# Differential attention: lambda and both softmax sums folded into one factor of the second component

## The chip, the cores and the metric

One core of a Trainium2 chip runs the whole program in one launch. The metric is device time in microseconds (us), the median of several executions.

## The reference, cut to what matters

Two layers of a backbone over 1024 latent and 256 context tokens. A part of each layer is differential attention with four heads. Each head has two components, and the second one's probabilities are subtracted with a factor lambda:

```python
s = jnp.einsum("bqhcd,bkhcd->bhcqk", q, k).astype(F32)
p = jax.nn.softmax(s, axis=-1)
w = (p[:, :, 0] - lam * p[:, :, 1]).astype(v.dtype)
o = jnp.einsum("bhqk,bkhd->bqhd", w, v)
...
return (rmsnorm(o, subln_g) * (1.0 - lam_init))
```

`rmsnorm` divides each row of o, over the 128 value channels of its head, by the root of its mean square plus NORM_EPS = 1e-6. It follows that a factor common to a whole row of w drops out, as long as NORM_EPS is multiplied by the square of that factor. In layer 0 latent and context queries are wanted, in layer 1 the latent ones alone.

## The kernel before, in words

The work of attention is cut into units: a head `hd`, a block `qb` of 256 queries and one half `qt` of it, 128 queries, against all 1280 keys. Block 0 is the context: its two halves make one unit, against 256 keys. Layer 0 has 36 units, layer 1 has 32. A software pipeline runs over steps s (the loop at L1310): in each step the operations of the list `K["ops"]` are issued, each for a unit that entered some steps before. For the unit that enters at step i:

- `qk` (L1188, step i): for each component TensorE makes 128 x 1280 scores in PSUM, a hi and a lo product of keys (L1209, L1210), VectorE takes the maximum (`tensor_reduce`, L1213), ScalarE the exponential, and adds up its row sum l as it goes (L1217). `u["l"]` holds l0 and l1 side by side.
- `weigh` (L1220, step i + 1): VectorE inverts both sums in one operation (L1223); GpSimd multiplies the second component, 128 x 1280, by 1/l1 and -lambda (L1226).
- `combine` (L1228, step i + 2): VectorE multiplies the first component by 1/l0 and adds the second (`scalar_tensor_tensor`, L1232).
- `trans` (L1234, step i + 3): TensorE transposes the ten 128 x 128 pieces (L1246); ScalarE and VectorE copy them to `wT` (L1247). The last two pieces go through the unused end of a score buffer.
- `pv` (L1249, step i + 4 of a block's second unit): 10 products with V for all 256 queries (L1256), in two parts; VectorE copies o (L1259).
- `subln` (L1262, steps i + 5 and i + 6): GpSimd squares o (L1267), TensorE sums the squares over the partitions with a matrix of ones (L1272), ScalarE takes logarithm and exponential for the root (L1274, L1275), VectorE scales o (L1279), and SyncE stores it (L1280).

While a head runs, `prep` loads the next head's K and Q and splits them into a rounded and a rest part: ScalarE rounds (`act.copy`, L139 and L1169), GpSimd subtracts (L140 in `split`, L1170), VectorE for head 0 alone. In the first steps `adaln_step` (L415) also puts matmuls of the conditioning in. Scores use two PSUM buffers, everything else on TensorE in this stage two banks.

GpSimd's instructions are held in the order in which they are written, over the whole program. On TensorE, VectorE and ScalarE the scheduler of the language chooses the order in the attention stage; the masks `cp` and `cd` fix it in other stages only. TensorE works its matmuls in fp32 here: one instruction of 256 or 128 columns in `pv` and `subln` shows as two records with a weight load each, a score product or a transpose as one.

Of the kernel before, what the change touches and what calls it, by code (L numbers as in the profile page):

```python
# [10 lines left out]
AF = mybir.ActivationFunctionType  # L11
ALU = mybir.AluOpType
AX = mybir.AxisListType

P = 128
# [8 lines left out]
EPS = 1e-6  # L24
# [52 lines left out]
def kernel(ctx: ExitStack, tc: tile.TileContext, I, out):  # L77
    nc = tc.nc
    sy = nc.sync
    dve = nc.vector  # L80
    act = nc.scalar
    pool = nc.gpsimd
    pe = nc.tensor
# [7 lines left out]
    def nm(s):  # L91
        uid[0] += 1
        return f"{s}{uid[0]}"
# [17 lines left out]
    def bank(shape, tag="b"):  # L111
        if TAGS[0] is not None:
            tag = "D" if tag == "b" else tag
            return PS[0].tile(shape, F32, tag=tag, name=nm(tag), bufs=TAGS[0][tag])
        return PS[0].tile(shape, F32, tag="b", name=nm("b"))
# [45 lines left out]
    def alternate(*gens):  # L161
        gens = list(gens)
        while gens:
            for g in list(gens):
                got = next(g, None)
                if got is None:
                    gens.remove(g)
                else:
                    yield got

    def tick(g, other, n):

        for got in g:
            run(g_lim(other, n))
            yield got
# [153 lines left out]
    ident = const.tile([P, P], F32, name="ident")  # L329
# [12 lines left out]
    ones = const.tile([P, P], F32, name="ones")  # L342
    epsc = const.tile([P, 1], F32, name="epsc")
# [38 lines left out]
    prmT, nlam = [], []  # L382
# [233 lines left out]
    for l in range(DEPTH):  # L616
        ps = bank([P, P])
        pe.transpose(ps[:, 0:NROW], prm_rows[:, l, :], ident[0:NROW, 0:NROW])
        t = const.tile([P, NROW], F32, name=nm("prm"))
# [111 lines left out]
    for l in range(DEPTH):  # L731
# [49 lines left out]
        def rgx_unit(ch):  # L781
            return conv_unit(lambda j: R_RCW + 2 * j + ch, R_RCB + ch, pt, lambda cv: RGS.__setitem__(("x", ch), cv), "xc")

        def rgg_unit(ch):
            G = rgt("G")
            RGS["g", ch] = G

            def evac(b, ps):
                s0, n = BLK[b]
                o = s0 if b == "c" else s0 + GAP  # L790
                act.activation(G[:, o:o + n], ps, AF.Gelu_apprx_tanh)

            return unit(X, ob, evac)
# [89 lines left out]
        u = alternate(rgx_unit(0), rgg_unit(0))  # L883
        put = gated(chain(*[store_h(b) for b in ("cab" if l == 0 else "b")]))
        u = tick(u, put, K["st"])
# [250 lines left out]
        def att(shape, tag, bufs=1, dt=F32, pl=None):  # L1136
            return (pl or AT[1]).tile(shape, dt, tag=tag, name=nm(tag), bufs=bufs)

        AT[0] = at0
        HD = {}  # L1140
# [37 lines left out]
        units = []  # L1178
# [9 lines left out]
        def qk(i, c, extra=None):  # L1188
# [26 lines left out]
            for a, (_, cc, _) in enumerate(parts):  # L1215
                p = pt_[cc][:, a // 2 * nk:(a // 2 + 1) * nk]
                act.activation(p, s[:, a, :], AF.Exp, bias=u["m"][:, c + a:c + a + 1], accum_out=u["l"][:, c + a:c + a + 1])  # L1217
                u["p"].append(p)

        def weigh(i):  # L1220
            u = U[i]
            n = len(u["p"])
            dve.reciprocal(u["l"][:, 0:n], u["l"][:, 0:n])  # L1223
            for a in range(1, n, 2):
                p = u["p"][a]
                pool.tensor_scalar(p, p, u["l"][:, a:a + 1], nlam[l], ALU.mult, ALU.mult)  # L1226

        def combine(i):  # L1228
            u = U[i]
            for a in range(0, len(u["p"]), 2):  # L1230
                p0, p1 = u["p"][a:a + 2]
                dve.scalar_tensor_tensor(p0, p0, u["l"][:, a:a + 1], p1, ALU.mult, ALU.add)  # L1232

        def trans(i, g, ext=None):  # L1234
            hd, qb, qt = units[i]
# [26 lines left out]
        def subln(i, part):  # L1262
            hd, qb, _ = units[i]
            o = HD["o", hd, qb]
            if part == 0:
                sq = att([P, 256], "sq", 2)
                pool.tensor_tensor(sq, o, o, ALU.mult)  # L1267
                HD["s", hd, qb] = sq
                return
            if part == 1:  # L1270
                sp_ = bank([P, 256])
                pe.matmul(sp_, ones, HD["s", hd, qb], start=True, stop=True)  # L1272
                rs = att([P, 256], "rs", 2)
                act.activation(rs, sp_, AF.Ln, scale=1.0 / P, bias=epsc)  # L1274
                act.activation(rs, rs, AF.Exp, scale=-0.5)  # L1275
                HD["r", hd, qb] = rs
                return
            rs = HD["r", hd, qb]
            dve.scalar_tensor_tensor(o, o, par[l]["gs"], rs, ALU.mult, ALU.mult)  # L1279
            sy.dma_start(mixD[4 + hd][:, qb * 256:(qb + 1) * 256], o)  # L1280
# [29 lines left out]
        for s in range(nu + 7):  # L1310
            if s < nu and s % per == 0 and units[s][0] < 3:
                todo = prep(units[s][0] + 1)
            e0 = (lambda ps=None: trans(s - 3, 2, ps)) if isu(s - 3) and units[s - 3][1] else None
            for op in K["ops"][l]:
                if op == "L0" and second(s - 5): subln(s - 5, 0)
                if op == "T0" and isu(s - 3): trans(s - 3, 0)
                if op == "T1" and isu(s - 3): trans(s - 3, 1)
                if op == "W" and isu(s - 1): weigh(s - 1)
                if op == "Q0" and isu(s): qk(s, 0, e0)
                if op == "Q1" and isu(s): qk(s, 1)  # L1320
                if op == "C" and isu(s - 2): combine(s - 2)
                if op == "P0" and second(s - 4): pv(s - 4, 0)
                if op == "P1" and second(s - 4): pv(s - 4, 1)
                if op == "E0" and e0 and not isu(s): e0()
                if op == "E1" and second(s - 5): subln(s - 5, 1)
                if op == "L2" and second(s - 6): subln(s - 6, 2)
                if op == "X" and todo: todo.pop(0)()
                if op in ("X", "Q1") and s < 3:
                    for _ in range(2):
                        adaln_step(ada1, None, True)  # L1330
            if s == 2:
                adaln_end()
# [230 lines left out]
        for fp in range(NF // 2):  # L1563
            if fp:
                t = xq.tile([P, 4, 512], F32, tag="hb", name=nm("s"), bufs=2)
# [102 lines left out]
        for d in range(0, KD, 2):  # L1668
            for b in ob:
                s0, n = BLK[b]  # L1670
# [166 lines left out]
```

## Time and profile before

| | |
|---|---|
| median of 3 runs | 3146.4 us (3146.09 to 3148.56) |
| the profiled execution's own time | 3146.0 us |
| its span in the profile | 3143.6 us |
| PE busy | 3012.1 us (96%) |
| DVE busy | 2035.5 us (65%) |
| ACT busy | 1376.6 us (44%) |
| POOL busy | 388.2 us (12%) |
| granted TensorE clock, mean | 0.982 of full speed |
| attention of layer 0 | about 468 to 706 us of the span |
| attention of layer 1 | about 2111 to 2330 us of the span |

PE is TensorE, PEld its weight loads, DVE VectorE, ACT ScalarE, POOL GpSimd, SP the queue of SyncE. Busy times are shares of the whole span and hide that a stage can have another limit than the program. Within attention three parts are told apart below: the head (the first units, beside loads and conditioning), the body, and the tail (no more scores, only the last units' transposes, value products and sub-norms).

### The profile page before, as it was taken

To read this page: it belongs to the slowest core of one execution; us is meant where nothing else is said; L and a number is where in the kernel's file an instruction comes from. 1 tells how busy PE (TensorE), PEld (TensorE's weight loads), DVE (VectorE), ACT (ScalarE), POOL (GpSimd) and SP (SyncE) were. 2 spreads that over 40 slices of the span, in tenths; PEclk is the share of its full clock that TensorE was granted. 3 is DMA by queue.
4 is the path that set the end of the run, shared out by engine and by line. 5 is a ranking of instruction groups with operands and counts; after the bars stand their busy time and mean duration, and the time that the engine had idled before them with its cause. 6 is when DMAs were issued, how large, how long until landed. Compare 5 with 4: busy or idle time off the path is not lost. (4 is left out here: it accounts for less than half of the span.)

```text
span 3143.6 us, 41895 instructions
## 1 busy us (share of the span) xinstructions
PE 3012.1 (96%) x15825; PEld 2472.4 (79%) x15825; DVE 2035.5 (65%) x3088; ACT 1376.6 (44%) x2491; POOL 388.2 (12%) x386
## 2 busy tenths in 40 slices
PE   6999998999999999999999799999989899999998
PEld 4888776778778778888888688877878688887887
DVE  5744657976764455557777664668966766666777
ACT  6643746765432323232212545746744433333122
POOL 1113114532000000000000013115421000000000
PEclk8999999999999999999999999999999999999999
DMA  9127565208233332225222224344124122225331
GB/s 310 57 79 212 176 175 143 67 17 265 69 116 127 115 122 73 81 67 198 91 76 76 70 86 124 112 137 133 39 101 151 54 81 81 81 83 197 95 94 61
DMA packets 327441, 353.11 MB, mean 112 GB/s; under 512 B 22237, under 2 KB 269382, under 8 KB 327238
## 3 DMA queue, kind: packets, MB, share of 16 engines
q1 hardware_dynamic: 327062, 350.36, 36.0%
q8 instruction: 124, 2.03, 0.3%
q14 instruction: 79, 0.65, 0.1%
q10 hardware_dynamic: 176, 0.07, 0.0%
HBM read 268.05 MB, written 82.31 MB: 111 GB/s over the span
## 5 line engine op out<-in xcount | busy, mean ns | idle before, releaser
L139 ACT CAST wo<-wr 128x512 fp32r<-128x512 f32 x374 | 230.2, 620 | 459.4 <-issue 145.2
L1464 PE MATMUL A<-x,wo 128*128 128x512 f32 x1584 | 392.2, 396 | 7.2 <-DVE wo L140 5.1
L1656 DVE SCALAR_TENSOR_TENSOR h<-b,mod,h 128x512 f32<-128x512 f32 (+1 forms) x456 | 301.4, 677 | 123.9 <-PE b L123 113.6
L140 DVE TENSOR_TENSOR wo<-wr,wo 128x512 fp32r<-128x512 f32 x374 | 253.9, 688 | 191.8 <-ACT wo L139 189.2
L1464 PEld LDWEIGHTS A<-x,wo 128*128 128x128 f32 x1584 | 294.3, 188 | 81.8 <-issue 7.5
L122 PE MATMUL b<-hl,wo 128*128 128x512 f32 (+1 forms) x912 | 333.9, 367 | 3.2 <-DVE hl L140 3.1
L121 PE MATMUL b<-hh,wo 128*128 128x512 f32 (+1 forms) x912 | 333.2, 366 | 3.6 <-ACT hh L139 3.4
L123 PE MATMUL b<-hh,wo 128*128 128x512 f32 (+1 forms) x912 | 332.3, 365 | 0.0
L123 PE MATMUL b<-xh,wl 128*128 128x512 f32 (+1 forms) x864 | 312.4, 362 | 11.6 <-DVE wl L140 11.6
L121 PE MATMUL b<-xh,wh 128*128 128x512 f32 (+1 forms) x864 | 317.9, 368 | 5.5 <-ACT xh L139 4.2
L122 PE MATMUL b<-xl,wh 128*128 128x512 f32 (+1 forms) x864 | 312.5, 362 | 7.1 <-DVE xl L490 4.2
L1464 PE MATMUL B<-x,wo 128*128 128x512 f32 x1056 | 263.9, 396 | 8.3 <-DVE x L140 5.6
L1464 PEld LDWEIGHTS B<-x,wo 128*128 128x128 f32 x1056 | 196.9, 189 | 57.8 <-DVE x L140 10.9
L1217 ACT ACTIVATE p<-s,m 128x1280 f32<-128x1280 f32 (+1 forms) x144 | 177.2, 1233 | 69.0 <-DVE m L1213 62.3
L121 PEld LDWEIGHTS b<-hh,wo 128*128 128x128 f32 x912 | 171.8, 189 | 35.8 <-ACT hh L139 5.0
L122 PEld LDWEIGHTS b<-hl,wo 128*128 128x128 f32 x912 | 172.3, 189 | 34.6 <-DVE hl L140 4.9
L1213 DVE TENSOR_REDUCE m<-s 128x1 f32<-128x1280 f32 (+1 forms) x132 | 190.5, 1472 | 10.6 <-PE s L1210 10.6
L121 PEld LDWEIGHTS b<-xh,wh 128*128 128x128 f32 x864 | 166.4, 193 | 38.2 <-issue 5.1
L123 PEld LDWEIGHTS b<-hh,wo 128*128 128x128 f32 x912 | 172.3, 189 | 28.6
L122 PEld LDWEIGHTS b<-xl,wh 128*128 128x128 f32 x864 | 164.9, 191 | 36.6 <-DVE xl L490 4.4
L123 PEld LDWEIGHTS b<-xh,wl 128*128 128x128 f32 x864 | 165.0, 191 | 35.7 <-DVE wl L140 12.1
L1209 PE MATMUL s<-kh,qs 128*128 128x512 f32 (+1 forms) x400 | 156.6, 393 | 23.8 <-ACT p L1217 20.8
(332 smaller groups left out, 5958.7 us busy)
## 6 DMA issues: line engine op xcount, KB each, us to landing
aw<-in_w_mod_dram SPq DMA_DIRECT2D x96, 512.0 KB, 4.9
wr<-in_w_in_dram SPq DMA_DIRECT2D x44, 512.0 KB, 3.9
wr<-in_w_gate_dram SPq DMA_DIRECT2D x44, 512.0 KB, 3.9
wr<-in_w_up_dram SPq DMA_DIRECT2D x44, 512.0 KB, 3.8
hid<-s SPq DMA_DIRECT2D x44, 512.0 KB, 2.6
wr<-in_w_down_dram SPq DMA_DIRECT2D x44, 512.0 KB, 3.2
t<-hid SPq DMA_DIRECT2D x88, 256.0 KB, 3.1
wr<-in_w_out_dram SPq DMA_DIRECT2D x40, 512.0 KB, 4.3
```

The lines of the kernel that those rows point to most:

```text
L121: pe.matmul(o, wh, xh, start=first, stop=False)
L122: pe.matmul(o, wh, xl, start=False, stop=False)
L123: pe.matmul(o, wl, xh, start=False, stop=last)
L139: act.copy(hi, src)
L140: lagged(lambda: (lo_eng or dve).tensor_tensor(lo, src, hi.bitcast(F32), ALU.subtract), key)
L1209: pe.matmul(s[:, a, k0:k0 + w], D["qs"][:, cc, tq:tq + P], D["kh"][:, cc, k0:k0 + w], start=True, stop=False)
L1213: dve.tensor_reduce(u["m"][:, c:c + n], s, AX.X, ALU.max, negate=True)
L1217: act.activation(p, s[:, a, :], AF.Exp, bias=u["m"][:, c + a:c + a + 1], accum_out=u["l"][:, c + a:c + a + 1])
L1464: pe.matmul(o, w[x][:, k, :], r[y][:, k, :], start=first and k == 0 and i == 0, stop=k == 3 and i == 2, skip_group_check=True)
L1656: dve.scalar_tensor_tensor(hv, ps, sect(l, 5, b, d), hv, ALU.mult, ALU.add)
```

## The change

The row of weights is multiplied by l0, which the sub-norm takes out again: p0 + (-lambda l0/l1) p1 takes the place of p0/l0 - lambda p1/l1. `weigh` now works on VectorE alone, with three operations on one element a partition: EPS x 128 x l0 squared into `le`, 1/l1, and -lambda l0/l1. `combine` scales the second component instead of the first. In the sub-norm, EPS can't be the same for all queries any more: per half of 128 queries, a second matmul adds EPS x 128 x l0 squared of each query to the sum of squares, with the column `le` broadcast as weights and the identity as moving operand. The constant bias of the logarithm goes.

```diff
+        LE = {}
+
         def weigh(i):
             u = U[i]
             n = len(u["p"])
-            dve.reciprocal(u["l"][:, 0:n], u["l"][:, 0:n])
-            for a in range(1, n, 2):
-                p = u["p"][a]
-                pool.tensor_scalar(p, p, u["l"][:, a:a + 1], nlam[l], ALU.mult, ALU.mult)
+            hd, qb, qt = units[i]
+            l0, l1 = u["l"][:, 0:n:2], u["l"][:, 1:n:2]
+            if (hd, qb) not in LE:
+                LE[hd, qb] = att([P, 2], "le", 6)
+            le = LE[hd, qb][:, 0:2] if qb == 0 else LE[hd, qb][:, qt:qt + 1]
+            dve.scalar_tensor_tensor(le, l0, EPS * P, l0, ALU.mult, ALU.mult)
+            dve.reciprocal(l1, l1)
+            dve.scalar_tensor_tensor(l1, l0, nlam[l], l1, ALU.mult, ALU.mult)
 
         def combine(i):
             u = U[i]
             for a in range(0, len(u["p"]), 2):
                 p0, p1 = u["p"][a:a + 2]
-                dve.scalar_tensor_tensor(p0, p0, u["l"][:, a:a + 1], p1, ALU.mult, ALU.add)
+                dve.scalar_tensor_tensor(p0, p1, u["l"][:, a + 1:a + 2], p0, ALU.mult, ALU.add)
...
             if part == 1:
                 sp_ = bank([P, 256])
-                pe.matmul(sp_, ones, HD["s", hd, qb], start=True, stop=True)
+                for t in range(2):
+                    c = slice(t * P, t * P + P)
+                    pe.matmul(sp_[:, c], ones, HD["s", hd, qb][:, c], start=True, stop=False)
+                    pe.matmul(sp_[:, c], LE[hd, qb][:, t:t + 1].to_broadcast([P, P]), ident, start=False, stop=True)
                 rs = att([P, 256], "rs", 2)
-                act.activation(rs, sp_, AF.Ln, scale=1.0 / P, bias=epsc)
+                act.activation(rs, sp_, AF.Ln, scale=1.0 / P)
```

## Rows read from the trace of the kernel before

**Rows 1.** Busy us by stretch: length, PE, PEld, DVE, ACT, POOL; clock, DMA, GB/s.

```profile
2111.57:2141.00 29.43, 18.64 (x111) 10.74 (x110) 20.86 (x16) 12.85 (x17) 13.57 (x6) 0.77 0.65 186
508.00:690.00 182.00, 175.20 (x968) 147.02 (x967) 160.03 (x183) 133.37 (x240) 88.21 (x61) 1.00 0.21 52
2141.00:2240.00 99.00, 96.86 (x541) 82.57 (x540) 89.04 (x101) 76.05 (x123) 54.16 (x32) 1.00 0.34 89
2240.00:2309.00 69.00, 68.65 (x389) 59.56 (x388) 61.77 (x72) 49.35 (x84) 24.30 (x19) 1.00 0.07 22
```

**Rows 2.** PE's groups, 508 to 690 us: count | busy us, mean ns | idle before.

```profile
L1256 PE MATMUL b<-wT,v 128*128 128x256 f32 x296 | 69.8, 380 | 0.1
L1209 PE MATMUL s<-kh,qs 128*128 128x512 f32 x105 | 47.0, 447 | 4.5 <-ACT p L1217 4.1
...
L1246 PE MATMUL b<-ident,p 128*128 128x128 f32 x236 | 36.9, 277 | 2.0 <-DVE p L1232 0.6 <-DVE o L1259 0.5 <-ACT wT L1247 0.4
L1209 PE MATMUL s<-kh,qs 128*128 128x256 f32 x69 | 19.2, 287 | 0.0
...
L1272 PE MATMUL b<-sq,ones 128*128 128x256 f32 x34 | 10.7, 397 | 0.2
L1246 PE MATMUL s<-ident,p 128*128 128x128 f32 x54 | 10.3, 272 | 0.0
```

**Rows 3.** PE in order of time, layer 1: start us, duration us, instruction.

```profile
2285.05 0.40 PE L1210 MATMUL s<-kl,qs 128*128 128x512 f32 x1
2285.28 0.27 PE L1209 MATMUL s<-kh,qs 128*128 128x256 f32 x1
...
2285.51 2.32 PE L1256 MATMUL b<-wT,v 128*128 128x256 f32 x10
2287.67 0.60 PE L1246 MATMUL b<-ident,p 128*128 128x128 f32 x4
```

**Rows 4.** Weight loads: sub-norm (min/median/max ns), and SSD state in order of time.

```profile
L1272 PEld LDWEIGHTS b<-sq,ones x72: 186/188/193, 517.2 to 2328.3; 128*128 128x128 f32 x72
...
270.38 0.97 PEld L964 LDWEIGHTS b<-xt,BW 128*128 128x128 f32 x8
```

**Rows 5.** PE in order of time, the last sub-norm of layer 1.

```profile
2328.19 0.70 PE L1272 MATMUL b<-sq,ones 128*128 128x256 f32 x2 [1.21 <-POOL sq L1267]
```

**Rows 6.** DVE's combining step, 508 to 690 us, then 2141 to 2309 us.

```profile
L1232 DVE SCALAR_TENSOR_TENSOR p<-p,l,p 128x1280 f32<-128x1280 f32 x29 | 51.1, 1763 | 3.8 <-POOL p L1226 3.6
...
L1232 DVE SCALAR_TENSOR_TENSOR p<-p,l,p 128x1280 f32<-128x1280 f32 x28 | 45.0, 1608 | 2.8 <-POOL p L1226 2.7
```

**Rows 7.** DVE, then POOL, in order of time, around 540 us.

```profile
538.97 0.17 DVE L1223 RECIPROCAL l<-l 128x2 f32<-128x2 f32 x1 [1.16 <-ACT p L1217]
...
539.68 2.88 DVE L1213 TENSOR_REDUCE m<-s 128x1 f32<-128x1280 f32 x2
542.83 4.21 DVE L1232 SCALAR_TENSOR_TENSOR p<-p,l,p 128x1280 f32<-128x1280 f32 x1 [0.27 <-POOL p L1226]
...
538.47 2.93 POOL L140 TENSOR_TENSOR kl<-raw,kh 128x1280 fp32r<-128x1280 f32 x1
...
542.76 2.93 POOL L140 TENSOR_TENSOR kl<-raw,kh 128x1280 fp32r<-128x1280 f32 x1
```

**Rows 8.** DVE in order of time, head of layer 1.

```profile
2125.93 4.18 DVE L1232 SCALAR_TENSOR_TENSOR p<-p,l,p 128x1280 f32<-128x1280 f32 x1 [1.55 <-POOL p L1226]
```

**Rows 9.** DVE in order of time, two steps late in layer 1.

```profile
2284.01 0.42 DVE L1247 COPY wT<-s 128x256 f32<-128x256 f32 x1 [0.17 <-PE s L1246]
...
2287.15 1.54 DVE L1232 SCALAR_TENSOR_TENSOR p<-p,l,p 128x1280 f32<-128x1280 f32 x1
...
2289.70 0.42 DVE L1247 COPY wT<-s 128x256 f32<-128x256 f32 x1 [0.59 <-PE s L1246]
```

**Rows 10.** DVE in order of time, a chain of small dependent operations.

```profile
98.42 1.38 DVE L362 SCALAR_TENSOR_TENSOR t<-t,t 128x8 f32<-128x8 f32 x7
99.83 0.17 DVE L363 SCALAR_TENSOR_TENSOR t<-t,t 128x8 f32<-128x8 f32 x1
```

## The prediction

> **What bounds the kernel now.** The change touches only the two attention stretches, some 238 and 219 us of the profiled span, so I read those and leave the rest alone. The views, in order: first the busy times by stretch, which say which engine has no room. In the head of layer 1's attention TensorE is busy for 18.6 of 29.4 us, at a mean granted clock of 0.77, that is partly at 1.2 instead of 2.4 GHz, and something else sets the pace. In the body it is nearly full: 175.2 of 182 us in layer 0, 96.9 of 99 and 68.65 of 69 us in layer 1, with VectorE at about nine tenths [rows 1]. The end of a matmul is modelled, so a busy PE can hide short idle times. The second view therefore counts records by shape, and the third gives the distance from one record to the next: 0.23 us for 512 columns of the score product, half of that for 256, (2.32 - 0.38)/9 = 0.216 us for a record of the value product, (0.60 - 0.28)/3 = 0.11 us for a transpose [rows 2, 3]. In the body of layer 0 this makes 296 x 0.216 + 210 x 0.23 + 138 x 0.115 + 290 x 0.11 + 34 x 0.216 = 167 us of work that TensorE cannot avoid (the lo products, one line further on, have the counts of the hi ones). So 15 of 182 us there are open; in the last 69 us of layer 1, where the record says 0.35 us, hardly any is. There TensorE is the bound. Where the next head's K and Q are split on GpSimd, VectorE, delayed, is late for TensorE.
>
> **What the change adds to TensorE.** The old sub-norm is one matmul over 256 columns, two records, 2 x 0.216 = 0.43 us. The new one is, for each half of 128 columns, ones times the squares and the broadcast l0 column times the identity: four matmuls of 128 columns in the same type, eight records. No record of before has exactly this form (full weights, 128 columns, two records a matmul), so it is bounded. Below: eight records at the 0.107 us of a 128-column transpose, 0.86 us. Above: each record waits out its weight load of 0.188 us, 1.50 us. The nearest row is the chunk state of the SSD part, full weights and 64 columns: eight weight loads in 0.97 us, (0.97 - 0.19)/7 = 0.11 us from one to the next, so a load that lasts 0.188 us holds up its neighbour by no more than that [rows 4]. I take 8 x 0.11 = 0.88 us, 0.45 us more for each of the 72/2 = 36 sub-norms; the ends are 0.43 and 1.07. A gain is excluded, TensorE only gets work.
>
> Where it falls: 6 sub-norms lie in the last 69 us of layer 1, where nothing is open: +2.7 us. 17 lie in the body of layer 0 and 7 in the first 99 us of layer 1's, 10.8 us of work; these stretches have idle time, but most of it comes in a few gaps and a sub-norm need not fall into one. I let a third vanish: +7.2 us. In the two tails there are 6; there the chain runs through TensorE alone, as the last one shows, for which PE and all behind it wait [rows 5]. Two of layer 0 follow each other closely and share one delay: 5 x 0.45 = +2.2 us.
>
> **What it removes.** The 72 products leave GpSimd's queue, and with them VectorE's wait before the combining step: 3.6 us in the body of layer 0 and 2.7 in that of layer 1 [rows 6]. What is late next is TensorE, so I book half, -3.2 us (between -6.3 and nothing).
>
> The combining step itself is slow at times: undisturbed it takes 1.54 us [rows 9], on average 1.763 and 1.608, so 29 x 0.22 + 28 x 0.07 = 8.3 us are lost [rows 6]. The reason stands in the timeline: at 542.76 the second K split begins on GpSimd, 0.07 us later the combining step that had waited for the product, and it ends only 4.21 us later, 2.9 of them the split [rows 7]. But the split, not the product, blocks it, and the splits stay. Without the product in between, the second split starts at about 541.4 instead of 542.76; the step, free at 542.56, would still meet it and lose 1.8 instead of 2.7 us. Against that, the new product of l0 and the reciprocal reads two SBUF operands too, and stands where the reciprocal stood at 539.0, in the middle of the first split, which runs until 541.4: a block of 2.4 us in front of two reductions that today go through. I book nothing, between -8.3 (no block left) and +9 us (a new block of 2.2 us at each of the four later head changes).
>
> In the head of layer 1 the same meeting costs 4.18 - 1.54 = 2.64 us, after a wait of 1.55 us for the product [rows 8]. Here the split can start before the combining step is due, since the product no longer holds it back. Of these 4.2 us I book 2.6, since the reductions behind must also wait for their scores and the split may now meet the new small operations; the ends are -4.2 and 0. The wait of PE's new matmuls for l0 squared costs nothing: VectorE writes it four steps before. GpSimd's squaring of o no longer stands behind products, which gives nothing, since PE reaches the sub-norm later. Dropping the bias from the logarithm moves nothing; the buffers change their release by nothing, since the combining step still reads the same tiles last. No DMA, and no order on SP's queue, is touched.
>
> **What it adds to VectorE.** Two operations of one element a partition per unit, 144 in all. A chain of seven dependent small ones runs from 98.42 to 99.83, 0.20 us each [rows 10]; that is 0.4 us a unit, 28.8 us in all; the lower end is nothing, where a wait covers them. The cover is the wait for TensorE's transposes that comes before the copy of wT: 0.17 us in one step, 0.59 in the next, so together 0.76 of the 0.8 us needed are there today [rows 9]. With 0.45 us more on TensorE in these two steps it is covered. Where a split has made VectorE late, that cover is gone; I book +2.0 us, between 0 and 14 (half of all of them).
>
> **Sum**: 2.7 + 7.2 + 2.2 - 3.2 + 0 - 2.6 + 2.0 = +8.3 us on the profiled execution, whose own time is 3146.0 us with a span of 3143.6. That is 3154.3; the median of the runs is 3146.4, so the two agree within 0.4 us, and I give 3154 us.
>
> **Rivals.** First, the other side: VectorE is set free. If every wait and every block above goes, 6.3 + 8.3 + 4.2 = 18.8 us are won, and if at the same time half of the sub-norms of the stretches with idle time vanish in it, TensorE's bill is 2.7 + 5.4 + 2.2 = 10.3 us: net -8.5, 3137.5 us. Its place is the combining step beside the K and Q splits; it is faster by more than a measurement can tell if over 16.6 of the 18.8 us are won. For it: every long combining step has a GpSimd instruction beside it. Against it: in rows 7 the blocker is the split. The Trainium skill, page "SBUF — State Buffer", section "SBUF: two separate sides", says that GpSimd and VectorE hold a common port pair exclusively, for a whole instruction, and that the loser blocks fully; by that rule alone fewer GpSimd instructions mean fewer blocks, which is this rival's time. The trace agrees on the block (4.21 us for 1.54), but a short operation with two SBUF inputs would block as well.
>
> Second, VectorE becomes the bound: the chain of three small operations is paid in half of the units, 14.4 instead of 2.0 us: 3167 us. For it: VectorE is at nine tenths; against it: the 0.17 and 0.59 us of idle. The Trainium skill, "VectorE: DVE Perf Modes", section "Rules for kernel authors", asks to keep the number of VectorE operations small, since each pays its drain; by that rule this rival has the better case. The trace agrees that such an operation costs 0.2 us however little it does.
>
> Third, the sub-norms of the bodies fit into idle time after all: 7.2 us less, 3147 us, no change that shows. Or the records of 128 columns wait for their weights: 36 x (1.07 - 0.45) = 22 us more, 3176 us; rows 4 speak against that, and I give it no chance of its own.
>
> **How the numbers follow.** About 0.2%, 6.3 us, is what a measurement of this kernel can tell from no change. Forecast (+2 to +14 us): 0.52, of which 0.34 lie above 6.3 us and 0.18 below. VectorE set free: 0.24, of which 0.22 faster. VectorE the bound: 0.11, slower. Fits into idle time: 0.13, no change. So faster 0.22, same 0.18 + 0.02 + 0.13 = 0.33, slower 0.34 + 0.11 = 0.45. The range reaches down into the first rival, to 3139 us, and up to most of the second, 3166 us; outside are about 0.09 below and 0.08 above. The forecast's own range is 3148 to 3160 us.
>
> **What would show it.** TensorE: eight records per sub-norm, 0.11 us apart; in the last steps of layer 1, two steps at 11.7 us would become 12.1. VectorE: no wait for GpSimd in front of the combining step; its mean still above 1.54 us where splits run; the product of l0 and the reciprocal long beside a split. The head of layer 1: no combining step over 4 us. Wrong would be: a body of layer 1 that is shorter than today, sub-norm records further apart than 0.15 us, or VectorE idle before the copy of wT while PE waits for it.

## The result, and the profile after

The changed kernel takes 3179.9 us (median of 4 runs, 3178.97 to 3182.47) against 3146.5: a ratio of 1.0104, 95% interval 1.0092 to 1.0115. It is slower by 33.4 us, where +8 were forecast and the range ended at +20. The profiled execution took 3180.1 us, its span is 3178.3 us.

The time is lost between the first and the last score product of each layer. In layer 0 that stretch was 219.0 us long and is now 241.5, in layer 1 it was 197.2 and is now 208.2: together 33.5 us. Everything else, both tails included, adds 1.2 us to the span.

The busy times by stretch, for the stretches that answer to [rows 1] (length, PE, PEld, DVE, ACT, POOL; clock, DMA, GB/s): body of layer 0, and the two parts of that of layer 1.

```profile
508.00:713.00 205.00, 186.52 (x1059) 160.90 (x1058) 178.09 (x240) 132.00 (x238) 36.35 (x26) 0.95 0.17 44
2165.00:2273.00 108.00, 98.55 (x571) 84.25 (x570) 97.62 (x127) 73.75 (x119) 26.04 (x17) 1.00 0.28 74
2273.00:2343.00 70.00, 68.88 (x407) 60.37 (x406) 63.30 (x92) 46.30 (x79) 4.76 (x6) 1.00 0.06 19
```

TensorE has now 18.5 of 205 us open in the body of layer 0 and 9.5 of 108 in layer 1, where it had 6.8 of 182 and 2.1 of 99. So of the 23.0 us by which the body of layer 0 grew 11.7 are waiting, and in the first part of layer 1's 7.3 of 9.0. The rest is busy time: the sub-norms are longer, and in layer 0 the mean granted clock is 0.95, where it was 1.00.

TensorE's new sub-norm, in order of time, answers to [rows 3, 4]. The pairs follow each other by 0.22 us, so eight records at 0.11 us, 0.89 us in all, as the prediction had it.

```profile
2205.07 0.39 PE L1282 MATMUL b<-sq,ones 128*128 128x128 f32 x2
2205.29 0.39 PE L1283 MATMUL b<-ident,le 128*128 128x128 f32 x2
...
2205.96 1.25 PE L1264 MATMUL b<-wT,v 128*128 128x256 f32 x5
```

VectorE's groups that answer to [rows 6], first 508 to 713 us, then 2165 to 2343 us (count | busy us, mean ns | idle before). L1240 is the combining step (its first line counts the form over all keys alone), L1234 the new product -lambda l0/l1, L1233 the reciprocal.

```profile
L1240 DVE SCALAR_TENSOR_TENSOR p<-p,l,p 128x1280 f32<-128x1280 f32 x27 | 52.5, 1943 | 0.4
...
L1234 DVE SCALAR_TENSOR_TENSOR l<-l,lw 128x1 f32<-128x1 f32 (+1 forms) x30 | 13.1, 437 | 0.8
...
L1233 DVE RECIPROCAL l<-l 128x1 f32<-128x1 f32 (+1 forms) x30 | 4.8, 161 | 15.0 <-ACT p L1217 14.6
...
L1240 DVE SCALAR_TENSOR_TENSOR p<-p,l,p 128x1280 f32<-128x1280 f32 x28 | 43.2, 1542 | 0.0
L1234 DVE SCALAR_TENSOR_TENSOR l<-l,lw 128x1 f32<-128x1 f32 x28 | 19.8, 709 | 0.9
...
L1233 DVE RECIPROCAL l<-l 128x1 f32<-128x1 f32 x27 | 4.4, 164 | 15.8 <-ACT p L1217 14.1
```

The wait for GpSimd before the combining step is gone, and in layer 1 its long runs too (1542 ns on average, which is undisturbed). In layer 0 it is slower than before, 1943 ns on average against 1763: 27 x 0.40 = 10.9 us over the undisturbed 1.54, where 6.4 were lost. And the product on one element a partition, 0.22 us when undisturbed, takes 437 and 709 ns on average: 30 x 0.217 + 28 x 0.489 = 20.2 us of standing still. And there is a wait of VectorE that the kernel before did not have to this extent, 14.6 and 14.1 us for the exponential (5.9 and 6.6 before).

The place of [rows 7], the change from head to head in layer 0: VectorE in order of time, then GpSimd.

```profile
537.70 0.16 DVE L1233 RECIPROCAL l<-l 128x1 f32<-128x1 f32 x1 [0.54 <-ACT p L1217]
537.90 2.91 DVE L1234 SCALAR_TENSOR_TENSOR l<-l,lw 128x1 f32<-128x1 f32 x1
540.84 4.15 DVE L1240 SCALAR_TENSOR_TENSOR p<-p,l,p 128x1280 f32<-128x1280 f32 x1
544.92 0.41 DVE L1255 COPY wT<-s 128x256 f32<-128x256 f32 x1
...
537.88 5.77 POOL L140 TENSOR_TENSOR kl<-raw,kh 128x1280 fp32r<-128x1280 f32 x2
```

The small product stands for the whole first K split, the combining step for the whole second one. Then come the copy of wT and the maximum: in the kernel before, the maxima went first, in the time of the first split. What that does to TensorE stands in its timeline:

```profile
548.23 0.80 PE L1209 MATMUL s<-kh,qs 128*128 128x512 f32 x1 [4.85 <-ACT p L1217]
548.82 0.63 PE L1210 MATMUL s<-kl,qs 128*128 128x512 f32 x1
549.25 0.63 PE L1209 MATMUL s<-kh,qs 128*128 128x512 f32 x1
```

And in the busy times of short stretches, columns as above:

```profile
546.00:548.00 2.00, 0.00 (x0) 0.00 (x0) 2.00 (x2) 1.24 (x2) 0.00 (x0) 0.74 0.85 195
548.00:550.00 2.00, 1.77 (x4) 1.48 (x5) 0.94 (x5) 2.00 (x6) 0.00 (x0) 0.50 0.21 68
...
552.00:554.00 2.00, 2.00 (x8) 1.69 (x7) 0.93 (x2) 1.42 (x2) 0.00 (x0) 0.56 0.00 0
```

A score buffer comes free when its exponential is done, the exponential needs the maximum, and the maximum was late. TensorE does nothing for 4.85 us, the granted clock falls to 0.50, that is 1.2 GHz, and a score product of 512 columns then needs 0.43 us (548.82 to 549.25) where it needed 0.23.

The second thing to see is the order on VectorE. Before the change a step ran, nearly throughout the body, as copy of wT, two maxima, combining step; the maxima between the copy at 2284.01 and the combining step at 2287.15 of [rows 9]:

```profile
2284.36 2.88 DVE L1213 TENSOR_REDUCE m<-s 128x1 f32<-128x1280 f32 x2
```

The changed kernel, in two late steps of layer 1, where no split runs:

```profile
2310.76 0.16 DVE L1233 RECIPROCAL l<-l 128x1 f32<-128x1 f32 x1 [1.09 <-ACT p L1217]
...
2311.43 2.88 DVE L1213 TENSOR_REDUCE m<-s 128x1 f32<-128x1280 f32 x2
2314.22 1.54 DVE L1240 SCALAR_TENSOR_TENSOR p<-p,l,p 128x1280 f32<-128x1280 f32 x1
...
2316.76 1.55 DVE L1240 SCALAR_TENSOR_TENSOR p<-p,l,p 128x1280 f32<-128x1280 f32 x1
2318.22 0.42 DVE L1255 COPY wT<-s 128x256 f32<-128x256 f32 x1
2318.55 2.88 DVE L1213 TENSOR_REDUCE m<-s 128x1 f32<-128x1280 f32 x2
```

Now every second combining step stands in front of the next copy and the next two maxima: two of them close together, then a step of 5.03 us with none (2306.40 to 2311.43 from maximum to maximum) in which VectorE waits 1.09 us, then one of 7.12 us. Nobody wrote this order: the scheduler of the language chose it. Which part of the change led it there these rows do not show; e4 below bears on that. Nor is it in these late steps that the order costs much: two of them take 12.15 us, and 12.03 in e2 below, which differs from the change by the kept order alone. The loss lies in the steps beside the splits.

### The profile page after: what moved, and what is told of

Its sections match the earlier page's. It is cut to its first block, busy times and chain, and to the rows that moved or that the text cites. A ratio compares the mean times of both kernels' runs of the same rounds, so it can differ in the third digit from the quotient of the medians.

```text
span 3178.3 us, 42342 instructions
## 1 busy us (share of the span) xinstructions
PE 3031.9 (95%) x16041; PEld 2496.8 (79%) x16041; DVE 2072.9 (65%) x3224; ACT 1375.2 (43%) x2491; POOL 281.0 (9%) x314
## 5 line engine op out<-in xcount | busy, mean ns | idle before, releaser
L1475 PEld LDWEIGHTS B<-x,wo 128*128 128x128 f32 x1056 | 197.5, 190 | 57.4 <-DVE x L140 10.7
L123 PEld LDWEIGHTS b<-xh,wl 128*128 128x128 f32 x864 | 165.4, 191 | 35.7 <-DVE wl L140 12.1
```

The lines of the kernel that those rows point to most:

```text
L123: pe.matmul(o, wl, xh, start=False, stop=last)
L1475: pe.matmul(o, w[x][:, k, :], r[y][:, k, :], start=first and k == 0 and i == 0, stop=k == 3 and i == 2, skip_group_check=True)
```

## The experiments

Three theories stood against each other: **A**, the new small products with two SBUF tensors are blocked by GpSimd's splits; **B**, the order of the combining steps on VectorE; **C**, TensorE's longer sub-norm. In the table, L0 and L1 are the times from first to last score product in the profile.

| kernel | median us | ratio to before (95% interval) | L0 | L1 |
|---|---|---|---|---|
| the change | 3179.9 | 1.0104 (1.0092 to 1.0115) | 241.5 | 208.2 |
| e1: small products with one tensor | 3169.2 | 1.0064 (1.0049 to 1.0079) | 232.0 | 207.0 |
| e2: order kept | 3155.5 | 1.0024 (1.0014 to 1.0033) | 224.6 | 200.4 |
| e3: e1 and e2 | 3145.2 | 0.9991 (0.9982 to 1.0001) | 219.1 | 196.1 |
| e8: before, order kept | 3144.7 | 0.9990 (0.9981 to 0.9999) | 220.3 | 192.9 |
| e5: e8 with the new sub-norm | 3160.1 | 1.0037 (1.0025 to 1.0050) | 231.3 | 198.7 |
| e4: e5, order left to the scheduler | 3193.1 | 1.0147 (1.0133 to 1.0161) | 238.8 | 222.7 |
| e7: e3 with the old sub-norm | 3140.6 | 0.9978 (0.9969 to 0.9987) | 218.2 | 191.6 |
| e6: e3 with a cheaper sub-norm | 3142.5 | 0.9984 (0.9975 to 0.9992) | 217.3 | 194.2 |
| e9: e6, le on ScalarE | 3142.5 | 0.9988 (0.9979 to 0.9997) | 217.5 | 194.7 |

### e1: the small products with one tensor as input

```diff
-            dve.scalar_tensor_tensor(le, l0, EPS * P, l0, ALU.mult, ALU.mult)
             dve.reciprocal(l1, l1)
-            dve.scalar_tensor_tensor(l1, l0, nlam[l], l1, ALU.mult, ALU.mult)
+            for a in range(0, n, 2):
+                l0a, l1a = u["l"][:, a:a + 1], u["l"][:, a + 1:a + 2]
+                dve.tensor_scalar(le[:, a // 2:a // 2 + 1], l0a, l0a, EPS * P, ALU.mult, ALU.mult)
+                dve.tensor_scalar(l1a, l1a, l0a, nlam[l], ALU.mult, ALU.mult)
```

> The changed kernel, with the two small products of each unit (EPS x 128 x l0 squared, and -lambda l0/l1) written as operations with one SBUF tensor as input and the other factor as a scalar per partition, instead of two SBUF tensors. Theory A (the new small two-input products meet GpSimd's splits and squares and stand still for a whole instruction): the excess that these lines show beside GpSimd instructions, about 10 us in layer 0 and 13 us in layer 1, goes, in part refilled by combining steps: 3160 to 3168 us. Theory B (the order on VectorE: without the product between them two combining steps run back to back, then none for a step, so that every second step VectorE stands idle for the exponential and the other one is too long): this edit leaves that order, so 3176 to 3183 us. Theory C (TensorE's longer sub-norm alone): 3180 us.

Measured: 3169.2 us, 10.7 less than the change; theory A, whose figure was missed by 1 us. VectorE, then GpSimd, at a Q split of layer 0:

```profile
561.16 0.16 DVE L1232 RECIPROCAL l<-l 128x1 f32<-128x1 f32 x1 [1.22 <-ACT p L1217]
561.36 0.27 DVE L1236 TENSOR_SCALAR l<-l,lw 128x1 f32<-128x1 f32 x1
561.55 2.32 DVE L1292 SCALAR_TENSOR_TENSOR o<-o,gs,rs 128x256 f32<-128x256 f32 x1
...
560.66 2.93 POOL L1170 TENSOR_TENSOR qs<-raw,qs 64x1280 fp32r<-64x1280 f32 x1
```

The same product, with the second factor as a scalar per partition, starts 0.70 us into the split and is done in 0.27 us, as everywhere: all 72 take 0.26 to 0.28 us. Right behind it the scaling of o, which reads two SBUF tensors, stands 2.32 us beside the same split, for 0.48 undisturbed. So block A is real and costs 10.7 us; two thirds of the loss are left. What is left is seen here, VectorE in layer 1 just after a combining step that had met a Q split:

```profile
2196.90 2.90 DVE L1242 SCALAR_TENSOR_TENSOR p<-p,l,p 128x1280 f32<-128x1280 f32 x1
...
2200.62 1.54 DVE L1242 SCALAR_TENSOR_TENSOR p<-p,l,p 128x1280 f32<-128x1280 f32 x1
2202.08 0.42 DVE L1257 COPY wT<-s 128x256 f32<-128x256 f32 x1
2202.41 1.48 DVE L1213 TENSOR_REDUCE m<-s 128x1 f32<-128x1280 f32 x1
...
2207.76 0.42 DVE L1269 COPY o<-b 128x256 f32<-128x256 f32 x1 [1.72 <-PE b L1266]
```

A second combining step, at 2200.62, comes ahead of the copy and the maxima. TensorE is busy for 0.42 of the 2.3 us from 2200.0; its mean granted clock is 0.70 from 2202.3 to 2204.3 and 0.65 from there to 2207.5, that is partly at 1.2 GHz; and then VectorE waits 1.72 us for TensorE.

### e2 and e3: the order kept, alone and with e1

```diff
             dve.tensor_reduce(u["m"][:, c:c + n], s, AX.X, ALU.max, negate=True)
+            u["red"] = list(tc.nc.cur_bb.bb.instructions)[-1].name
...
                 dve.scalar_tensor_tensor(p0, p1, u["l"][:, a + 1:a + 2], p0, ALU.mult, ALU.add)
+                if a == 0 and i + 1 in U:
+                    info = mybir.DependencyInfo(mybir.DependencyClass.NoSync, mybir.DependencyReason.DATA)
+                    tc.add_manual_dep(list(tc.nc.cur_bb.bb.instructions)[-1], U[i + 1]["red"], info, reason="program order")
```

The added line only tells the scheduler to place the combining step behind the next unit's last maximum; it adds no wait between engines. The other engines' order follows as the scheduler will.

> The changed kernel, with one thing added: the combining step of a unit is kept behind the last max reduction of the unit after it, which is the order in which VectorE ran them before the change. Theory B (order): most of the 33 us goes, 3150 to 3160 us. Theory A (blocks of the small two-input products): 3174 to 3186 us, since their meetings with GpSimd stay. Theory C (sub-norm on TensorE): 3180 us.

> The changed kernel with both edits: small products with one tensor input, and the combining step kept behind the next unit's last max reduction. Theory A or B, or the two together: what is left is TensorE's longer sub-norm, 8 to 16 us over the kernel before, 3152 to 3162 us. Theory C (the sub-norm on TensorE is what costs 33 us): 3180 us. If VectorE's blocks by GpSimd's splits had been the price of the Pool product in the kernel before, it comes below 3146 us.

Measured: e2 3155.5 us, 24.4 less than the change; e3 3145.2 us, 34.7 less, and within the interval no different from the kernel before. The two gains taken alone, 10.7 and 24.4, add up to 35.1. So the order is the larger part, the blocks the smaller, and with both undone the loss is gone, though the new sub-norm is still there: theory C, that TensorE's longer work is the price, falls. The figure for e3 was 7 us too high, since the 8 to 16 us expected for the sub-norm are not there. Its 3145.2 us also meet the last case of that text, below 3146 us; what the removed product is worth is taken up at e7.

By the table, the order is worth 16.9 us in layer 0 and 7.8 in layer 1 (e2 against the change), and 12.9 and 10.9 with the small products no longer blocked (e3 against e1).

In e2 the small product still stands, in the same place as in the change, VectorE and then GpSimd; but behind it come the maxima, not a combining step that meets the second split:

```profile
538.09 2.90 DVE L1235 SCALAR_TENSOR_TENSOR l<-l,lw 128x1 f32<-128x1 f32 x1
540.92 0.41 DVE L1259 COPY wT<-s 128x256 f32<-128x256 f32 x1
541.26 2.87 DVE L1213 TENSOR_REDUCE m<-s 128x1 f32<-128x1280 f32 x2
...
538.04 5.79 POOL L140 TENSOR_TENSOR kl<-raw,kh 128x1280 fp32r<-128x1280 f32 x2
```

In e3 the same head change costs TensorE nothing. Its busy times from 540 to 548 and from 548 to 600 us:

```profile
540.00:548.00 8.00, 8.00 (x48) 6.82 (x47) 7.90 (x9) 4.65 (x10) 5.24 (x2) 1.00 0.55 126
548.00:600.00 52.00, 51.37 (x306) 44.30 (x305) 47.91 (x71) 40.73 (x72) 15.86 (x9) 1.00 0.31 72
```

The same two stretches of the changed kernel:

```profile
540.00:548.00 8.00, 3.38 (x21) 2.83 (x20) 7.96 (x5) 2.04 (x4) 3.64 (x2) 0.93 0.69 164
548.00:600.00 52.00, 48.85 (x259) 42.01 (x260) 43.03 (x63) 34.99 (x63) 8.33 (x6) 0.88 0.20 51
```

8.00 against 3.38 us busy, and behind it a clock of 1.00 against 0.88. If the body's 0.95 is read as 1.00 and 0.50 in turns, a tenth of 205 us ran at half speed, which is at most 10 of layer 0's 22.5 us (an estimate; no run holds the clock apart from the idle time that goes before it).

The order costs without the clock as well. The body of layer 0 up to the last score product, in e1 and then in e3:

```profile
508.00:700.00 192.00, 179.52 (x1052) 154.27 (x1051) 170.56 (x244) 130.58 (x232) 41.21 (x26) 1.00 0.19 48
508.00:687.70 179.70, 178.25 (x1059) 154.83 (x1058) 162.64 (x245) 132.19 (x236) 37.67 (x25) 1.00 0.22 56
```

The clock is 1.00 in both, and e1, with the order free, is 12.3 us longer; TensorE is idle for 12.5 us there, and for 1.5 in e3.

### e5, e8 and e4: the sub-norm alone, its control, and its order

e5 is the kernel before with the new sub-norm (and a constant column EPS x 128) and the order kept; e8 only keeps the order, by the lines of e2; e4 is e5 without them.

```diff
+    lec = const.tile([P, 1], F32, name="lec")
...
+    dve.memset(lec, EPS * P)
...
-                pe.matmul(sp_, ones, HD["s", hd, qb], start=True, stop=True)
+                for t in range(2):
+                    c = slice(t * P, t * P + P)
+                    pe.matmul(sp_[:, c], ones, HD["s", hd, qb][:, c], start=True, stop=False)
+                    pe.matmul(sp_[:, c], lec.to_broadcast([P, P]), ident, start=False, stop=True)
```

> The kernel before, with the Pool product, the old row sum scaling and the old combining step, and only the new sub-norm: four matmuls of 128 columns, with a constant column EPS x 128 where the change has the column of EPS x 128 x l0 squared, and no bias in the logarithm; the combining step is kept in its old place on VectorE. Theories A and B: 36 sub-norms of 0.45 us at most, of which some vanish in idle time: 8 to 16 us over the kernel before, 3154 to 3162 us; the sum of the prediction had 12.1 us for it, 3158 us. Theory C: near 3180 us. If the sub-norms fit into idle time: 3146 to 3150 us.

> The control for e5: the kernel before with nothing but the combining step kept behind the next unit's last max reduction, where it nearly always stood anyway. Order as before, so 3144 to 3149 us. If it differs from the kernel before by more than 3 us, that difference has to be taken off e5's 13 us, and the order is a matter of its own in the kernel before too.

> The kernel of e5 (the kernel before with the new sub-norm alone, Pool product kept) without the edit that keeps the combining step in its place. The scheduler then draws about every second combining step of layer 1, and several of layer 0, in front of the copy of wT and the next unit's reductions. Theory B (the order costs, whatever small operations there are): 10 to 24 us more than e5, 3170 to 3184 us. If the order cost only together with the blocks of the new small products, or with the Pool product gone: as e5, 3158 to 3163 us.

Measured: e8 3144.7, e5 3160.1, e4 3193.1 us. Against its control the sub-norm costs 15.5 us in the kernel that still has the product, at the upper end of what was expected. Part of that is no work of TensorE: in the order that goes with it, the final scaling of o, which also reads two SBUF tensors, meets a split at two head changes, VectorE and then GpSimd:

```profile
562.27 3.05 DVE L1288 SCALAR_TENSOR_TENSOR o<-o,gs,rs 128x256 f32<-128x256 f32 x1
...
561.01 4.03 POOL L1172 TENSOR_TENSOR qs<-raw,qs 64x1280 fp32r<-64x1280 f32 x1
```

That is 3.05 - 0.48 = 2.6 us each time, 5 in all; in e8 one scaling takes 1.44 us and none longer. What makes up the other ten us is not taken apart.

e4 is 33 us slower than e5, by the order alone, and above the 10 to 24 that theory B had: the order costs in a kernel that has neither the new small products nor lost the GpSimd product. And the lost product is not needed for it: here the new sub-norm, an edit of TensorE's and ScalarE's work, was enough for the scheduler to draw the combining steps forward on VectorE, and together they cost 46.6 us over the kernel before, more than the whole change. What led the scheduler there in the changed kernel, the sub-norm, the lost product or both, stays open: no run leaves the order free in the change with the old sub-norm. Late in layer 1, where no split runs, VectorE and then TensorE:

```profile
2323.92 1.48 DVE L1215 TENSOR_REDUCE m<-s 128x1 f32<-128x1280 f32 x1
...
2327.10 1.55 DVE L1234 SCALAR_TENSOR_TENSOR p<-p,l,p 128x1280 f32<-128x1280 f32 x1 [0.23 <-POOL p L1228]
...
2330.59 1.55 DVE L1234 SCALAR_TENSOR_TENSOR p<-p,l,p 128x1280 f32<-128x1280 f32 x1 [1.24 <-POOL p L1228]
...
2332.39 2.88 DVE L1215 TENSOR_REDUCE m<-s 128x1 f32<-128x1280 f32 x2
...
2337.47 1.48 DVE L1215 TENSOR_REDUCE m<-s 128x1 f32<-128x1280 f32 x1
...
2335.43 0.50 PE L1211 MATMUL s<-kh,qs 128*128 128x512 f32 x1 [1.23 <-ACT p L1219]
```

The combining step that was drawn forward waits 1.24 us for the product, with the copy and two maxima queued behind it; TensorE then waits 1.23 us for an exponential. Two steps take 13.55 us (2323.92 to 2337.47), where e5 needs 12.04.

### e7, e6 and e9: what is left of the sub-norm

e7 puts the old sub-norm into e3 and so leaves the factor l0 squared of EPS out. e6 computes all of it with ones times the squares in one matmul and the addition in the type of the score products (`identr` is the identity in that type, and `le` has it too); e9 is e6 with `le` as a square on ScalarE. The edits of e7, e6 and e9, in this order:

```diff
-                for t in range(2):
...
+                pe.matmul(sp_, ones, HD["s", hd, qb], start=True, stop=True)
...
-                act.activation(rs, sp_, AF.Ln, scale=1.0 / P)
+                act.activation(rs, sp_, AF.Ln, scale=1.0 / P, bias=epsc)
```

```diff
-                for t in range(2):
-                    c = slice(t * P, t * P + P)
-                    pe.matmul(sp_[:, c], ones, HD["s", hd, qb][:, c], start=True, stop=False)
-                    pe.matmul(sp_[:, c], LE[hd, qb][:, t:t + 1].to_broadcast([P, P]), ident, start=False, stop=True)
+                pe.matmul(sp_, ones, HD["s", hd, qb], start=True, stop=False)
+                for t in range(2):
+                    c = slice(t * P, t * P + P)
+                    pe.matmul(sp_[:, c], LE[hd, qb][:, t:t + 1].to_broadcast([P, P]), identr, start=False, stop=(t == 1))
```

```diff
-                dve.tensor_scalar(le[:, a // 2:a // 2 + 1], l0a, l0a, EPS * P, ALU.mult, ALU.mult)
+                act.activation(le[:, a // 2:a // 2 + 1], l0a, AF.Square, scale=(EPS * P) ** 0.5)
```

> The kernel of e3 with the old sub-norm: one matmul of 256 columns and the constant EPS as bias of the logarithm. It leaves out the factor l0 squared of EPS, so its sub-norm is not the reference's; all else is e3. If the four matmuls cost here what they cost in e5 (13 us), 3129 to 3136 us; if they are hidden in e3, since VectorE sets the pace there, 3141 to 3146 us. The difference to the kernel before is then what the removal of the Pool product alone is worth with the order kept and the small products written with one tensor: about -15 us by the difference of e5 and e3.

> The kernel of e3 with a cheaper sub-norm that computes the same: ones times the squares in one matmul of 256 columns as before the change, and EPS x 128 x l0 squared added by two matmuls of 128 columns in the single-pass type that the score products have, one record each. By the 0.115 us that 256 columns of a score product took for one record, two of 128 take about 0.12 us, an estimate, where e3 pays 0.45: 3132 to 3138 us, faster than both kernels. If the change of type between matmuls costs a stop, or the sub-norm was hidden in e3: 3143 to 3147 us.

> The kernel of e6 with EPS x 128 x l0 squared computed by ScalarE as a square with a scale, 68 operations of one element, in place of VectorE's. VectorE has 68 x 0.20 = 13.6 us less work in the attention stages. Where VectorE sets the pace, around the head changes, some of it is won: 3134 to 3141 us; where TensorE does, nothing: 3141 to 3144 us. If each square keeps ScalarE's exponential or its copy of wT waiting, slower: up to 3155 us.

Measured: e7 3140.6, e6 3142.5, e9 3142.5 us, none as low as its lower figures; e7 and e6 lie between their two cases, nearer to the one in which the sub-norm is mostly hidden. From e7 to e3 the four matmuls cost 4.5 us, not 13. By the stretches of the table it is 0.9 us in layer 0, where TensorE's open time falls from 16.8 to 12.0 us, and 4.5 in layer 1 (what lies between the stretches differs by a few us from one execution to the next). The removed product is worth 4.0 us (e7 against e8), not the 15 that e7's text took from e5 and e3. The price for each sub-norm is right all the same: two late steps, from maximum to maximum, take 11.62 us in e7, 12.03 in e3, so 0.41 for a sub-norm. In e6 it is 0.18 (11.80 us), its sub-norm on TensorE:

```profile
2284.36 0.59 PE L1288 MATMUL b<-sq,ones 128*128 128x256 f32 x2
2284.60 0.52 PE L1291 MATMUL b<-identr,le 128*128 128x128 f32 x2
2284.95 1.29 PE L1272 MATMUL b<-wT,v 128*128 128x256 f32 x5
```

e6 computes what the change computes and is faster than both kernels, by 0.16% (0.08 to 0.25%) against the one before; e8, where nothing but the order is kept, is already 0.10% faster than that one, and the two intervals overlap. Taking `le` from VectorE wins nothing more: 30 squares of 0.207 us in layer 1 on ScalarE, and the same time.

## Why the prediction was wrong

**TensorE's price** was right: eight records 0.11 us apart, two late steps at 12.15 us where 12.1 stood (12.03 with the order kept). **What of it is paid** depends on the rest: 12.1 us were booked; 15.5 are paid beside the product, 4.5 in e3. The third rival, that the sub-norms of the bodies fit into idle time, holds for layer 0 in e3. In the tails +2.2 were booked; from the last score product to the last scaling of o they take 20.3 and 23.9 us, where they took 19.1 and 21.7, so +3.4, of which the sub-norm alone is 1.9 (e3 against e7). The chain there does not run "through TensorE alone": in [rows 5] TensorE waits 1.21 us for GpSimd's squares.

**The removed product and the head of layer 1**, -3.2 and -2.6, with +2.0 for the small operations, make -3.8. With the order kept and the sub-norm old, the difference is 3140.6 - 3144.7 = -4.0 us (e7 against e8; the intervals of the two overlap by a little). The three terms were not measured one by one, so their sum may fit by luck; and 68 units have 136 small operations, not the 144 that the prediction counted. In the changed kernel, too, no combining step in the head of layer 1 is longer than 1.55 us, as the prediction asked. The cover for the small operations went elsewhere: in layer 1 VectorE's idle time is now in front of the reciprocal, not of the copy of wT.

**The step that failed** is the one on the combining step at the splits: "a block of 2.4 us in front of two reductions that today go through", for which it says "I book nothing, between -8.3 (no block left) and +9 us (a new block of 2.2 us at each of the four later head changes)". It failed twice. The block had been named, with its place, the new product of l0 and the reciprocal in the middle of the first split, but it was put at nothing. It stands 2.91 us, not 2.4; in layer 1 it meets both K splits of a head change and the Q splits as well; it stands beside GpSimd's squares too. These blocks measured 20.2 us in the two bodies, and cost 10.7 with those of the other new product, `le` (e1 against the change). And it is not the reductions that stand behind the block: at 540.84 it is a combining step, which meets the second split.

The rule of the Trainium skill, "SBUF — State Buffer", section "SBUF: two separate sides", which the prediction weighed, is borne out by 537.90 (2.91 us for one element), and so is its condition on two SBUF inputs: with one tensor and a scalar per partition the same product takes 0.27 us. The first rival drew from that rule that fewer GpSimd instructions mean fewer blocks; what the trace shows is the reason that the prediction gave against it, that a short operation with two SBUF inputs blocks as well.

**What no step had** is that change of the order. Every term took VectorE's instructions in the sequence of [rows 7, 9], though the scheduler chooses it in this stage. That is 24.4 us (e2 against the change), the larger part of the miss, and 33 in e4. With it goes what the prediction had seen in the head alone, a granted clock below 1.00: at 548 us, after 4.85 us of idle time, it is at 1.2 GHz, and the late maximum is paid again in slower matmuls.

The second rival's 3167 us is nearer to the result, but for another reason: VectorE did not become the bound by three small operations' time, it stood 14.6 and 14.1 us waiting in the two bodies.

One way from the kernel before to the change, one part at a time, by medians: order kept 3146.5 to 3144.7, product gone to 3140.6, new sub-norm to 3145.2 (e3), small products of two tensors to 3155.5 (e2), free order to 3179.9. Only the last two steps are large. What stays open is which part of the change led the scheduler to the new order, how much of the last step the clock makes up beyond the idle time itself, and why keeping the order gains the 1.8 us in the kernel before (its interval reaches almost to no change).

## What to carry to other kernels

Where a scheduler orders an engine's queue, an edit anywhere in the stage can also be an edit of the order, as e4 shows, where TensorE's sub-norm moved VectorE's combining steps: compare the two orders first, and say in the program which order is meant. An operation of one element can cost what its neighbour on GpSimd costs if it reads two tensors from SBUF (2.91 us here); give the second factor as a scalar per partition. The price of work on a full engine is not what is paid: it has to be measured beside what else is late in that stage.

## What the runs showed of the hardware that was not expected

- A product of 128 x 1 elements stood 2.91 us beside a split of 2.92 us, the same product as a one-tensor operation took 0.27 us in the middle of one of 2.93 us (e1).
- A wait of TensorE was followed by a slower clock: after 4.85 us without a matmul, some 6 us at 0.50, with score products 0.43 us apart in place of 0.23; in the body of layer 0 the mean was 0.95, and 1.00 again in e3.
- Two matmuls of 128 columns in the type of the score products, added to a fp32 sum of 256 columns in the same bank, raise a step of two units by 0.18 us, in place of 0.41 for the fp32 form.
